# Cache copies, head states and the first output-projection weights in a hybrid decoder step

## The chip, the cores and the metric

The kernel runs on one core of a Trainium2 chip. The metric is the device time of one execution in microseconds (us). Before the change three runs gave 789.93, 790.48 and 792.44 us; the median is 790.48 us.

## The reference, cut to what matters

One layer is computed for 512 prompt tokens (one sequence) and for 8 sampled tokens (8 sequences with 1024 cached tokens each), with 1024 model dimensions and float32 results.

```python
sh_a, sc_a, gt_a, sh_f, sc_f, gt_f = adaln(c, w_ada[l], b_ada[l])
h = rms_norm(x, g_pre_mix[l]) * (1.0 + sc_a) + sh_a
parts = split_projection(h @ w_in[l])
o_nsa, o_hgrn, states = mixer(parts, l)
mixed = jnp.concatenate([rms_norm(o_nsa, g_nsa_out[l]), o_hgrn], axis=-1) @ w_out[l]
x = x + gt_a * rms_norm(mixed, g_post_mix[l])
h = rms_norm(x, g_pre_ffn[l]) * (1.0 + sc_f) + sh_f
ffn = hier_moe(h, w_route_group[l], b_route_group[l], ...)
x = x + gt_f * rms_norm(ffn, g_post_ffn[l])
```

`mixer` is two things side by side. `o_nsa` is a sparse attention with 8 heads of 64 (a compressed, a selected and a window branch, summed with gates). `o_hgrn` is a gated linear recurrence with 4 heads and a 128 x 128 state each, whose final state is an output. The window cache of the 8 sampled sequences is an output too: it is the old one moved on by one row. So 511 of its 512 rows per sequence are a plain copy, 511 KB for each of 8 sequences:

```python
kw = jnp.concatenate([win_buf, kv_w.astype(win_buf.dtype)], axis=1)
return nsa_combine(gates, o_c, o_s, o_w), kw[:, t:]
```

`hier_moe` sends each token to 2 of 16 experts, each a gated MLP with 256 hidden columns.

## The kernel before, in words

The program has stages in this order: modulation and norms, input projection, recurrence inputs and attention scores, the mixing proper, output projection, residual and router, routing, experts, final norm. A float32 product is made of three products of rounded numbers: each operand is split into a high part (a copy on ScalarE, ACT in the profile) and a low part (a subtraction, mostly on VectorE, DVE, some on GpSimd, POOL); `split`, L111 to L113, does that, and its two instructions carry the lines L112 and L113 wherever they are called.

The change lies in the mixing and in the start of the output projection.

**The mixing** (from about 330 to 447 us) runs several generators. Each `next` issues one step of one of them, and a string gives the order: `ORD_D`, then `ORD_F`, then `ORD_E`.

- `mix(h)`, h = 0 to 3, letters 4 to 7: one head of the recurrence over the prompt. It builds the state tile `S` (128 x 4 x 128, one for each of 4 chunks), L997 to L1000, stores the last one (`O["ph"]`, L1001, a DMA on SyncE's queue), multiplies with it (L1008), normalizes (L1011 to L1018; `hq` holds the head's output) and transposes the result into `mixT` (L1022, L1023).
- `attn(i)`, i = 0 to 3, letters a to d: attention of 128 prompt tokens. Scores go to the two PSUM tiles `mm`, their exponentials to a ring of three SBUF tiles `PT` (L1055), the values are summed in `ob` (L1066). At the end the squares of `ob` go to a tile `sqt` of its own (L1077, L1078), and four matmuls with ones sum them (L1081); the output is written as high and low parts `mh` (L1088, L1089).
- `hgrn_samples`, letter h: the recurrence of the 8 samples. It writes the values to DRAM (`HV`, L1107), reads them back broadcast to all partitions (`VB`, 2 MB, L1108), and updates the state tiles `S0` (printed as S too; L1102, L1125) two samples at a time. The last step normalizes `osn` and transposes it (L1146).
- `copy_windows`, letter w: the eight cache copies, one a step, DRAM to DRAM on SyncE's queue (L711).

**The output projection** (from L1171) takes `w_out` in eight tiles of 128 x 1024, 512 KB each. Tiles 0 to 3 hold the first 512 output columns, 4 to 7 the second 512. `load_wout` (L1174 to L1177) issues one load on SyncE's queue, into one of six slots `ewr0` to `ewr5` of the pool `wpa`, or later into `ewr6` to `ewr9` of the pool `res`. `wpa` is opened after the mixing's own pools (`hgo` with `hq`, `hl`, `hv`; `hmx`) are closed, at the same place in SBUF. `wout_half` (L1185) splits four tiles: the high part goes to `ewh` (first half) or `ewi` (second half), the low part to another slot. `first_half`, letter f in `ORD_E`, splits the first four, then loads tiles 4 and 5 into slots 2 and 3, then splits the four heads of `mixT` into `mhh`. Tiles 6 and 7 are loaded after `res` is opened. `wout` (L1269, matmuls at L1277) computes 128 tokens by 512 columns in 24 matmuls; `wout_samples` (L1290) the samples. `router_weights` (L1323 to L1350) prepares the router in small matmuls. `ORD_W` gives the order of these.

**What sets the order.** Outside of a few stretches that are written out by hand (routing and experts), the program's order is only a priority: a planner simulates the program with its own costs and sets the order of each engine's instructions. Each engine then runs its list in order. Transfers are issued by SyncE (SP) and by ACT, in order too; an issue that must wait holds up all behind it. `tc.keep_in_program_order` pins an instruction: what comes before it in the program on that engine is issued before it, and what comes after it is issued after it. A tile pool gives out tiles by name; `bufs` is how many a name has in rotation, and a tile may be written when all readers of what was in its place are done. DMA completions are told by eight semaphores that are given out in turn, over both queues.

Of the kernel before, what the change touches and what calls it, by code (L numbers as in the profile page):

```python
# [11 lines left out]
F32 = mybir.dt.float32  # L12
# [10 lines left out]
D = 1024  # L23
# [32 lines left out]
ORD_C = "PPPrPsPrPPrPsPrPPsPrPPrPsPrPPrsPPPrPsPrPPrttsPPrPPrsPPPrsPPrPPrsPPrPsPPrPPrsPPrttPsPrPPrPsPPrPsPrPPrPsPrPPsPrPPrPsPrttPPrsPPrPPsPrPPrsPPrPPrsPPPrsPPPPsPPPsPPPPPPPPPtt"  # L56
ORD_D = "gvvvvgvvvvgvvvv4vvvvv4vvvvv45vvvvv45vvvvv456vvvvv"
ORD_E = "dhfdhfdhfdhfdhdhdhdhdhdhhhh"
ORD_F = "h456waaha456w7abhb56w7bbhb5w67bchc6w7ccwhc67wcchcw7h7h"
ENG = "aadaaaaaddddddddddddddppppppddppppppaaaaddddadaappppaaaadpddppppppppaaaadaaadddddddddpppaaapadddddpddpppd"  # L60
ORD_W = "ffhhrlhhhlrfrgggaaaaalfagfllllglalaala"
ORD_M = "GLAESSTBKSSSSGLAEFLSSTBBBBKSSSSGLAEFLSSTBKSSSSGLAEFLSSTBKSSSSGLAEFLSSTBKSSGLAEFLSSTBKSSGLAEFLSSTBKGLAEFLSSTBKSSGLAEFLSSTKSSSSGLAEFLSSTKSSSSGLAEFLSSTKSSSSGLAEFLSSTKSSSSGLAEFLSSTKSSSSGLAEFLSSTKSSSSGLAEFLSSTKSSSSGLAEFLSSTKSSSSGLAEFLSSTKGLAEFLTK"
# [2 lines left out]
def body(tc, I, O):  # L65
    nc = tc.nc
    es = ExitStack()
    dve, act, pool, pe, sp = nc.vector, nc.scalar, nc.gpsimd, nc.tensor, nc.sync

    def stage():  # L70
        return es.enter_context(ExitStack())

    def open_pool(name, bufs, stack, side="left"):
        return stack.enter_context(tc.tile_pool(name=name, bufs=bufs, side=side, reuse_waits=REUSE))
# [13 lines left out]
    def ps_mm():  # L88
        return bank("mm", 2, 512)
# [7 lines left out]
    def ps_t():  # L97
        return bank("pt", 512)

    def ps_o():  # L100
        return bank("po", 512)
# [9 lines left out]
    def split(src, hi, lo, eng=None):  # L111
        act.activation(hi, src, AF.Copy)  # L112
        (eng or dve).tensor_tensor(lo, src, hi.bitcast(F32), op=ALU.subtract)  # L113
# [4 lines left out]
    def copied(i, dst, src):  # L118
        if ENG[i] == "a":
            act.activation(dst, src, AF.Copy)  # L120
        else:
            en(i).tensor_copy(dst, src)
# [585 lines left out]

    def copy_windows():
        for b in range(8):  # L710
            tc.keep_in_program_order(sp.dma_start(O["sw"][b], I["cwo"][b]))  # L711
            yield

    def drained(gens):
        for c, g in gens.items():
            assert next(g, self_end) is self_end, c
# [16 lines left out]
    def sample_attention():  # L733
# [50 lines left out]
        for r in range(2):  # L784
# [26 lines left out]
            for q in range(2):  # L811
                S = ps_t()
                for bb in range(4):
                    pe.matmul(S[32 * bb:32 * bb + 32, :], qb[:, 4 * r + bb, :], SLK[bb][:, 4 * q:4 * q + 4, :], start=True, stop=True)
                dve.tensor_tensor(P[:, 512 * q:512 * q + 512], S, ts[:, 512 * q:512 * q + 512], op=ALU.add)
            W = ps_t()
# [71 lines left out]
    hmx = open_pool("hmx", 1, s_hm)  # L888
# [52 lines left out]
    def mix(h):  # L941
# [52 lines left out]
        pk = ps_f()  # L994
        for c in range(4):
            pe.matmul(pk[:, 128 * c:128 * c + 128], KT_[:, c], hv[:, c, 128 * h:128 * h + 128], start=True, stop=True)
        S = hmx.tile([128, 4, 128], F32, name="S")  # L997
        copied(40 + h, S[:, 0], pk[:, 0:128])
        for c in range(1, 4):
            dve.scalar_tensor_tensor(S[:, c], S[:, c - 1], EB[:, c:c + 1], pk[:, 128 * c:128 * c + 128], op0=ALU.mult, op1=ALU.add)  # L1000
        sp.dma_start(O["ph"][:, h], S[:, 3])  # L1001
        yield
        po = ps_f()
        for c in range(4):
            o = po[:, 128 * c:128 * c + 128]
# [21 lines left out]
    gens = dict(v=hgrn_values(), g=gated_raw(), **{"4567"[h]: mx4[h] for h in range(4)})  # L1027
# [7 lines left out]
    s_at = stage()  # L1035
    at = open_pool("at", 1, s_at, "right")
# [4 lines left out]
    def attn(i):  # L1041
        qc = slice(128 * i, 128 * i + 128)
        ob = ps_o()
        last = []
        for h in range(8):
            o = ob[64 * (h % 2):64 * (h % 2) + 64, 128 * (h // 2):128 * (h // 2) + 128]
            pe.matmul(o, Vb[:, h // 4, h % 4, :], pcT[:, i, h // 4, :], start=(h < 2), stop=False)
        for g in range(2):
            def scores(n, j):
                S = ps_mm()  # L1050
                for br in range(2):
                    pe.matmul(S[:, br], AK[:, i, i - j], AG[:, 8 * br + 4 * g:8 * br + 4 * g + 4], start=True, stop=False)
                    for q in range(2):
                        pe.matmul(S[:, br], KS[g][:, q, br, j], QS[g][:, :, qc], start=False, stop=(q == 1))  # L1054
                PT = at.tile([128, 2, 4, 128], F32, name="PT", bufs=3)  # L1055
                S4 = S.rearrange("p b (h q) -> p b h q", h=4)
                for h in range(4):
                    act.activation(PT[:, :, h], S4[:, :, h], AF.Exp, scale=-SL[4 * g + h])  # L1058
                if n == 0:
                    pool.affine_select(out=PT, in_=PT, compare_op=ALU.is_ge, fill=0.0, base=0, pattern=[[0, 8], [1, 128]], channel_multiplier=-1)  # L1060
                return PT, g, j, n

            def values(PT, g, j, n):
                for br in range(2):
                    for par in range(2):
                        pe.matmul(ob[64 * par:64 * par + 64, 256 * g:256 * g + 256], VT[:, j, br, 64 * g:64 * g + 64],  # L1066
                                  PT[:, br].rearrange("p (r t) q -> p t r q", t=2)[:, par], start=False, stop=(n == i and br == 1 and g == 1))

            for n, j in enumerate([i, *range(i)]):
                s_ = scores(n, j)  # L1070
                if last:
                    values(*last.pop())
                last.append(s_)
                yield
        values(*last.pop())
        yield
        sqt = at.tile([128, 4, 128], F32, name="sqt")  # L1077
        act.activation(sqt, ob.rearrange("p (f q) -> p f q", f=4), AF.Square)  # L1078
        ps = ps_t()
        for f in range(4):  # L1080
            pe.matmul(ps[:, 0:1], sqt[:, f], ones[:, 0:1], start=(f == 0), stop=(f == 3))  # L1081
        copied(80 + i, ssn[:, i:i + 1], ps[:, 0:1])
        for f in range(4):
            src = ob[:, 128 * f:128 * f + 128]
            if ENG[76 + i] == "a":
                act.activation(mhi[f][:, qc], src, AF.Copy, scale=gn[:, f:f + 1])
            else:
                dve.tensor_scalar(mhi[f][:, qc], src, gn[:, f:f + 1], None, op0=ALU.mult)  # L1088
            dve.scalar_tensor_tensor(mlo[f][:, qc], src, gn[:, f:f + 1], mhi[f][:, qc].bitcast(F32), op0=ALU.mult, op1=ALU.subtract)  # L1089
        yield  # L1090
# [58 lines left out]

    hs = hgrn_samples()
    gens.update(h=hs, w=copy_windows(), **{"abcd"[i]: attn(i) for i in range(4)})
    with contextlib.ExitStack() as order:
        if DMAN:
            order.enter_context(tc.manual_schedule(engines={pe.engine}))
        for c in ORD_F:
            next(gens[c], None)
        drained({c: gens[c] for c in "abcw4567"})
        s_hm.close()  # L1160
        s_hg.close()

        wpa = open_pool("wpa", 1, es)
        slot = [lambda dt, c=c: wpa.tile([128, D], dt, name=f"ewr{c}") for c in range(6)]
        hslot = [lambda dt, c=c: wpa.tile([128, D], dt, name=f"ewh{c}") for c in range(4)]
        high = [h(F32R) for h in hslot]
        mh2 = [wpa.tile([128, D], F32R, name=f"mhh{c}") for c in range(4)]
        mhh, mlh = ([mh2[2 * q + h // 2][:, 512 * (h % 2):512 * (h % 2) + 512] for h in range(4)] for q in range(2))  # L1170
        KKS = (2, 3, 0, 1)  # L1171
        raw = []

        def load_wout(s_):  # L1174
            c = len(raw)
            raw.append(slot[s_](F32))
            sp.dma_start(raw[c], I["wo"][c // 4, KKS[c % 4]])  # L1177

        for c in range(4):
            load_wout(c)  # L1180

        def halves(x):
            return x.rearrange("p (a b) -> p a b", a=2)

        def wout_half(hf, wh, wl):  # L1185
            for q, kk in enumerate(KKS):
                c = 4 * hf + q
                lo = slot[(4, 5, 0, 1, 8, 9, 2, 3)[c]](F32R)
                split(raw[c], high[c], lo, en(93 + c))
                wh[kk], wl[kk] = halves(high[c]), halves(lo)  # L1190
                yield

        ws, wt2 = ([None] * 4, [None] * 4), ([None] * 4, [None] * 4)

        def first_half():
            for _ in wout_half(0, *ws):
                pass
            yield
            load_wout(2)
            load_wout(3)  # L1200
            for h in range(4):
                split(mixT[4 + h][:, 0:NP], mhh[h], mlh[h], en(101 + h))
                yield

        fh = first_half()
        play(ORD_E, h=hs, d=gens["d"], f=fh)
    s_at.close()
# [26 lines left out]
    high += [res.tile([128, D], F32R, name=f"ewi{c}") for c in range(4)]  # L1234
    slot += [lambda dt, c=c: res.tile([128, D], dt, name=f"ewr{c}") for c in range(6, 10)]
    ring = [gslot, *slot[6:8], *slot[0:2], *slot[4:6], *hslot, *slot[2:4]]
    load_wout(6)
    load_wout(7)
    loaded = []

    def load_next():
# [163 lines left out]
    raws, parts, at, used = {}, {}, {}, set()  # L1405
# [335 lines left out]
    with tc.manual_schedule(engines=MANUAL and {getattr(nc, e).engine for e in MANUAL}):  # L1741
# [5 lines left out]
        for o in ORD_M:  # L1747
            u = k[o] if o in k else 0
            if o in k:
                k[o] += 1  # L1750
                w, c = units[min(u, len(units) - 1)]
# [230 lines left out]
```

## Time and profile before

| what | value |
| --- | --- |
| median of three runs | 790.48 us |
| the profiled execution's own time | 791.27 us |
| its span, first to last instruction | 789.6 us |
| mean granted TensorE clock | 0.92 |
| TensorE busy, of the span | 651.7 us (83%) |
| VectorE, ScalarE, GpSimd busy | 464.0, 374.1, 183.3 us |
| moved by DMA | 160.81 MB, mean 204 GB/s |
| SyncE's queue | 125.98 MB, 46.6% of 16 engines' span |
| ScalarE's queue | 25.39 MB, 9.9% |
| the eight cache copies issued | from 359.7 to 456.4 us |
| the eight loads of w_out issued | from 462.1 to 475.9 us |

Times in the profile count from the first instruction of the span. "PE" is a matmul, "PEld" the load of its stationary operand, "SPq" and "ACTq" the issue of a transfer on that engine's queue. In a timeline each row gives the start, how long it took, the engine, the line, the operation, what it writes and reads, and in brackets how long the engine was idle before it and what ended that wait. A float32 matmul shows as two instructions. Rows of waits give what waited, for what, the total, how often, and the longest. The wait of an instruction for several things is put down to the last of them.

### The profile page before, as it was taken

The numbers are of one execution on the slowest core, as the hardware profiler recorded it, in microseconds if no ns is written. First come the engines' busy times: TensorE is split into PE (matmuls) and PEld (weight loads), VectorE is DVE, ScalarE is ACT, GpSimd is POOL, SyncE is SP. The second block draws the span as 40 slices with busy tenths as digits, with TensorE's granted clock in tenths as the row PEclk, the third lists the DMA queues.
The fourth block names the chain that finished last, engine by engine and source line by source line (L and its number), as shares of the span: only waits on it lengthen the run. The fifth ranks groups of instructions, "written<-read, shape, count | busy, mean of one in ns | idle before, by whom it ended". The sixth has DMA issues, their size and how long they took to land. (4 is left out here: it accounts for less than half of the span.)

```text
span 789.6 us, 13169 instructions
## 1 busy us (share of the span) xinstructions
PE 651.7 (83%) x4495; PEld 490.3 (62%) x4495; DVE 464.0 (59%) x1140; ACT 374.1 (47%) x759; POOL 183.3 (23%) x208
## 2 busy tenths in 40 slices
PE   3885988998999999897999739995288899999930
PEld 1663866687878788885676426564255577666620
DVE  4523613345867765577643544356865976888806
ACT  4212512334455547623444234445445766888723
POOL 1000310002130131425432112435301223222114
PEclk9898999999999999999999958997588999999975
DMA  8876798866454632106221485338698889998515
GB/s 302 262 256 218 258 315 295 316 197 205 141 175 130 182 118 73 56 4 262 94 81 55 102 303 177 112 123 319 212 358 295 263 222 287 359 333 296 148 29 213
DMA packets 74604, 160.81 MB, mean 204 GB/s; under 512 B 11346, under 2 KB 39538, under 8 KB 74146
## 3 DMA queue, kind: packets, MB, share of 16 engines
q1 hardware_dynamic: 59844, 125.98, 46.6%
q10 hardware_dynamic: 10654, 25.39, 9.9%
q0 software_dynamic: 4032, 8.53, 5.1%
q8 instruction: 37, 0.61, 0.3%
q14 instruction: 37, 0.30, 0.1%
HBM read 145.29 MB, written 24.28 MB: 215 GB/s over the span
## 5 line engine op out<-in xcount | busy, mean ns | idle before, releaser
L563 PE MATMUL pp<-hhi,wh 128*128 128x260 f32 x256 | 75.6, 295 | 0.3 <-ACT kvt L441 0.3
L563 PE MATMUL pp<-hlo,wh 128*128 128x260 f32 x256 | 74.4, 291 | 0.0
L563 PE MATMUL pp<-hhi,wl 128*128 128x260 f32 x256 | 74.2, 290 | 0.0
L1669 POOL DMA_INDIRECT Y<-ot,gi x17 | 24.4, 1438 | 130.1 <-ACT ot L1668 123.0
L563 PEld LDWEIGHTS pp<-hhi,wh 128*128 128x128 f32 x256 | 49.4, 193 | 2.7 <-issue 2.0
L563 PEld LDWEIGHTS pp<-hhi,wl 128*128 128x128 f32 x256 | 49.3, 193 | 2.4 <-issue 2.3
L563 PEld LDWEIGHTS pp<-hlo,wh 128*128 128x128 f32 x256 | 49.4, 193 | 1.4 <-issue 1.2
L655 ACT ACTIVATE jn<-P,M 128x128 bf16<-128x128 f32 (+3 forms) x64 | 35.9, 560 | 27.3 <-DVE M L653 21.8
L113 DVE TENSOR_TENSOR wl<-wr,wh 128x1024 fp32r<-128x1024 f32 x9 | 11.2, 1250 | 39.8 <-ACT wh L112 39.8
L1058 ACT ACTIVATE PT<-mm 128x256 f32<-128x256 f32 x80 | 23.9, 388 | 19.8 <-PE mm L1054 19.7
L1640 PE MATMUL pf<-ewi,xh 128*96 128x512 f32 x72 | 30.2, 419 | 2.0 <-ACT xh L112 2.0
L653 DVE CUSTOM_DVE_ANT_0 P<-mm,tb 128x128 f32<-128x128 f32 (+3 forms) x64 | 29.0, 483 | 4.0 <-PE mm L646 3.9
L397 PE MATMUL mm<-hhi,wh 128*128 128x260 f32 x144 | 29.9, 288 | 1.3 <-ACT wh L112 1.3
L1640 PE MATMUL pf<-ewi,xl 128*96 128x512 f32 x72 | 29.5, 409 | 1.2 <-DVE xl L113 1.2
L112 ACT ACTIVATE wh<-wr 128x1024 fp32r<-128x1024 f32 x9 | 9.5, 1057 | 43.3 <-DMA wr<-in_wi 25.9
L397 PE MATMUL mm<-hlo,wh 128*128 128x260 f32 x144 | 30.0, 285 | 0.0
L397 PE MATMUL mm<-hhi,wl 128*128 128x260 f32 x144 | 29.7, 287 | 0.0
L646 PE MATMUL mm<-ka,qs 128*128 128x512 f32 (+2 forms) x112 | 27.6, 354 | 0.1
L1054 PE MATMUL mm<-qs,ka 128*128 128x512 f32 x80 | 26.6, 405 | 0.0
L1667 ACT ACTIVATE ot<-mm 96x512 f32<-96x512 f32 x17 | 10.1, 594 | 33.3 <-PE mm L1664 33.3
L397 PEld LDWEIGHTS mm<-hhi,wh 128*128 128x128 f32 x144 | 22.2, 188 | 5.0 <-issue 3.4
L299 PEld LDWEIGHTS po<-cg,w1c 128*128 128x128 f32 x160 | 21.5, 214 | 5.7 <-issue 3.3
(651 smaller groups left out, 1885.1 us busy)
## 6 DMA issues: line engine op xcount, KB each, us to landing
ewr<-in_ew SPq DMA_DIRECT2D x37, 512.0 KB
wa<-in_wa SPq DMA_DIRECT2D x16, 1024.0 KB
wr<-in_wi ACTq DMA_DIRECT2D x25, 512.0 KB
ewt<-in_ew SPq DMA_DIRECT2D x24, 512.0 KB
cg<-in_cc SPq DMA_DIRECT2D x64, 128.0 KB
ewh<-in_ew SPq DMA_DIRECT2D x16, 512.0 KB
x<-in_ew SPq DMA_DIRECT2D x15, 512.0 KB
mh<-in_wa SPq DMA_DIRECT2D x13, 512.0 KB
```

Of the source, the lines that this page charges most:

```text
L113: (eng or dve).tensor_tensor(lo, src, hi.bitcast(F32), op=ALU.subtract)
L299: pe.matmul(p[:, 128 * k:128 * k + 128], w1c[:, k, s, :], cg[:, :, k, s, :], start=(s == 0), stop=(s == 7))
L397: pe.matmul(p[:, hf, 0:260], a[:, k, :], b[:, k, hf * 260:hf * 260 + 260], start=(k == 0 and j == 0), stop=(k == KT - 1 and j == 2))
L563: pe.matmul(p[:, 0:260], a[:, k, :], b[:, k, c], start=(k == 0 and j == 0), stop=(k == KT - 1 and j == 2))
L646: pe.matmul(o, QS[g][:, h % 4, qc], KA[g][:, j, a:b], start=(j == 0), stop=(j == 1))
L653: dve.tensor_tensor_reduce(out=p, in0=sb[:, br], in1=tb0[:, 384 - 128 * i:512].rearrange("p (k n) -> p k n", n=128), scale=SL[h], scalar=1 ...
L655: act.activation(jn[:, 0:128 * (i + 1)], p.rearrange("p k n -> p (k n)"), AF.Exp, scale=-1.0, bias=M[:, 0, i, br, h:h + 1], accum_out=M[:, ...
L1054: pe.matmul(S[:, br], KS[g][:, q, br, j], QS[g][:, :, qc], start=False, stop=(q == 1))
L1058: act.activation(PT[:, :, h], S4[:, :, h], AF.Exp, scale=-SL[4 * g + h])
L1640: pe.matmul(pg, a[:, k, :], b[:, wk_], start=(k == 0 and j == 0), stop=(k == 7 and j == 2))
L1667: act.activation(o3[:, 0], pd[:, 0], AF.Copy)
L1669: pool.indirect_dma_start(out=Y, out_offset=bass.IndirectOffsetOnAxis(ap=gix, axis=0), in_=ot, in_offset=None, bounds_check=T - 1, oob_is_ ...
```

## The change

Three things are changed.

- The eight copies are no longer pinned; they stand at other places of `ORD_F`.
- The state tile `S` of `mix` has two buffers instead of one. The squares `sqt` of `attn` no longer have a tile: they take half of a `PT` tile, from its ring of three.
- The first four tiles of `w_out` get four tiles of their own (`wq0` to `wq3`, 4 KB a partition each, in a pool opened on the right side, above the attention's). They are loaded by a new generator `first_weights`, letter o, two in the second step of `ORD_F` and two in the twelfth. Tiles 4 and 5 are loaded into slots 2 and 3 as soon as `wpa` is open. The order of the letters 4 to 7, a, b, c and h among themselves is the same.

```diff
--- before.py
+++ after.py
@@ -56,7 +56,7 @@
...
 ORD_D = "gvvvvgvvvvgvvvv4vvvvv4vvvvv45vvvvv45vvvvv456vvvvv"
 ORD_E = "dhfdhfdhfdhfdhdhdhdhdhdhhhh"
-ORD_F = "h456waaha456w7abhb56w7bbhb5w67bchc6w7ccwhc67wcchcw7h7h"
+ORD_F = "ho456aaha45ow67awwbhb567wwbbhb567bwwchc67wwcchc67cchc7h7h"
 ENG = "aadaaaaaddddddddddddddppppppddppppppaaaaddddadaappppaaaadpddppppppppaaaadaaadddddddddpppaaapadddddpddpppd"
 ORD_W = "ffhhrlhhhlrfrgggaaaaalfagfllllglalaala"
 ORD_M = "GLAESSTBKSSSSGLAEFLSSTBBBBKSSSSGLAEFLSSTBKSSSSGLAEFLSSTBKSSSSGLAEFLSSTBKSSGLAEFLSSTBKSSGLAEFLSSTBKGLAEFLSSTBKSSGLAEFLSSTKSSSSGLAEFLSSTKSSSSGLAEFLSSTKSSSSGLAEFLSSTKSSSSGLAEFLSSTKSSSSGLAEFLSSTKSSSSGLAEFLSSTKSSSSGLAEFLSSTKSSSSGLAEFLSSTKGLAEFLTK"
@@ -708,7 +708,7 @@
 
     def copy_windows():
         for b in range(8):
-            tc.keep_in_program_order(sp.dma_start(O["sw"][b], I["cwo"][b]))
+            sp.dma_start(O["sw"][b], I["cwo"][b])
             yield
 
     def drained(gens):
@@ -994,7 +994,7 @@
         pk = ps_f()
         for c in range(4):
             pe.matmul(pk[:, 128 * c:128 * c + 128], KT_[:, c], hv[:, c, 128 * h:128 * h + 128], start=True, stop=True)
-        S = hmx.tile([128, 4, 128], F32, name="S")
+        S = hmx.tile([128, 4, 128], F32, name="S", bufs=2)
         copied(40 + h, S[:, 0], pk[:, 0:128])
         for c in range(1, 4):
             dve.scalar_tensor_tensor(S[:, c], S[:, c - 1], EB[:, c:c + 1], pk[:, 128 * c:128 * c + 128], op0=ALU.mult, op1=ALU.add)
@@ -1074,7 +1074,7 @@
                 yield
         values(*last.pop())
         yield
-        sqt = at.tile([128, 4, 128], F32, name="sqt")
+        sqt = at.tile([128, 2, 4, 128], F32, name="PT", bufs=3)[:, 0]
         act.activation(sqt, ob.rearrange("p (f q) -> p f q", f=4), AF.Square)
         ps = ps_t()
         for f in range(4):
@@ -1149,14 +1149,29 @@
 
 
 
+    raw = []
+    KKS = (2, 3, 0, 1)
+
+    def load_wout(t_):
+        c = len(raw)
+        raw.append(t_)
+        sp.dma_start(t_, I["wo"][c // 4, KKS[c % 4]])
+
+    def first_weights():
+        wq = open_pool("wq", 1, s_at, "right")
+        for c in range(4):
+            load_wout(wq.tile([128, D], F32, name=f"wq{c}"))
+            if c % 2:
+                yield
+
     hs = hgrn_samples()
-    gens.update(h=hs, w=copy_windows(), **{"abcd"[i]: attn(i) for i in range(4)})
+    gens.update(h=hs, o=first_weights(), w=copy_windows(), **{"abcd"[i]: attn(i) for i in range(4)})
     with contextlib.ExitStack() as order:
         if DMAN:
             order.enter_context(tc.manual_schedule(engines={pe.engine}))
         for c in ORD_F:
             next(gens[c], None)
-        drained({c: gens[c] for c in "abcw4567"})
+        drained({c: gens[c] for c in "abcow4567"})
         s_hm.close()
         s_hg.close()
 
@@ -1168,16 +1183,8 @@
         high = [h(F32R) for h in hslot]
         mh2 = [wpa.tile([128, D], F32R, name=f"mhh{c}") for c in range(4)]
         mhh, mlh = ([mh2[2 * q + h // 2][:, 512 * (h % 2):512 * (h % 2) + 512] for h in range(4)] for q in range(2))
-        KKS = (2, 3, 0, 1)
-        raw = []
-
-        def load_wout(s_):
-            c = len(raw)
-            raw.append(slot[s_](F32))
-            sp.dma_start(raw[c], I["wo"][c // 4, KKS[c % 4]])
-
-        for c in range(4):
-            load_wout(c)
+        load_wout(slot[2](F32))
+        load_wout(slot[3](F32))
 
         def halves(x):
             return x.rearrange("p (a b) -> p a b", a=2)
@@ -1196,8 +1203,6 @@
             for _ in wout_half(0, *ws):
                 pass
             yield
-            load_wout(2)
-            load_wout(3)
             for h in range(4):
                 split(mixT[4 + h][:, 0:NP], mhh[h], mlh[h], en(101 + h))
                 yield
@@ -1234,8 +1239,8 @@
     high += [res.tile([128, D], F32R, name=f"ewi{c}") for c in range(4)]
     slot += [lambda dt, c=c: res.tile([128, D], dt, name=f"ewr{c}") for c in range(6, 10)]
     ring = [gslot, *slot[6:8], *slot[0:2], *slot[4:6], *hslot, *slot[2:4]]
-    load_wout(6)
-    load_wout(7)
+    load_wout(slot[6](F32))
+    load_wout(slot[7](F32))
     loaded = []
 
     def load_next():
```

## The prediction

> **What bounds the kernel now.** I began with the page: it says which stage has slack on TensorE, and what clock it was granted there.
>
> ```profile
> PE   3885988998999999897999739995288899999930
> PEclk9898999999999999999999958997588999999975
> DMA  8876798866454632106221485338698889998515
> ```
>
> A slice is 19.7 us. TensorE is nearly full except where the page shows a hole near 455 to 475 us (the 3 in the PE row, a 5 in the clock row) and a second one at the routing. To read the first hole I asked for stretches.
>
> ```profile
> 430.00:440.00 10.00, 10.00 (x57) 6.40 (x56) 0.60 (x1) 4.23 (x13) 2.13 (x2) 1.00 0.00 0
> 440.00:450.00 10.00, 5.70 (x53) 2.71 (x52) 7.41 (x33) 3.37 (x11) 1.18 (x9) 1.00 0.48 109
> 450.00:460.00 10.00, 8.23 (x67) 6.65 (x67) 5.14 (x30) 2.99 (x6) 1.65 (x2) 0.56 0.70 191
> 460.00:470.00 10.00, 1.46 (x4) 0.60 (x4) 3.11 (x7) 1.08 (x2) 2.25 (x2) 0.50 1.02 346
> ```
>
> The columns are PE, PEld, DVE, ACT, POOL, granted clock, DMA share and GB/s. From 430 to 440 the DMA engines move nothing; from 460 to 470 they are full and every compute engine is nearly idle. Work that could have been fetched earlier is fetched while all wait. The timeline names it.
>
> ```profile
> 445.43 0.33 PE L1022 MATMUL pt<-ident,hq 128*128 128x128 f32 x1
> ...
> 450.86 0.30 PE L1146 MATMUL pt<-ident,osn 128*128 128x128 f32 x1 [3.61 <-DVE osn L1143]
> ...
> 451.16 0.34 SPq L1001 DMA_DIRECT2D out_ph<-S  x1
> 451.54 5.41 SPq L711 DMA_DIRECT2D out_sw<-in_cwo  x2
> ...
> 460.11 0.24 PE L1331 MATMUL po<-sel,lT 128*8 128x20 f32 x2 [0.29 <-DVE lT L1330]
> ...
> 462.13 14.09 SPq L1177 DMA_DIRECT2D ewr<-in_wo  x8
> ...
> 467.52 1.06 ACT L112 ACTIVATE ewh<-ewr 128x1024 fp32r<-128x1024 f32 x1 [7.69 <-DMA ewr<-in_wo]
> 468.63 1.22 PE L1277 MATMUL mm<-ewh,mhh 128*128 128x512 f32 x2 [8.28 <-ACT ewh L112]
> ...
> 471.24 4.62 DVE L113 TENSOR_TENSOR ewr<-ewr,ewh 128x1024 fp32r<-128x1024 f32 x4
> ...
> 472.52 0.80 PE L1277 MATMUL mm<-ewr,mhh 128*128 128x512 f32 x1 [2.67 <-DVE ewr L113]
> ```
>
> The mixing ends near 446, small router matmuls run from 450.86 to 460.35, and then the output projection (L1277) waits 8.28 us for its first weight tile and 2.67 us for the low part of it. The queue's own waits say why the eight loads come only at 462.13.
>
> ```profile
> SPq L1001 <- DMA tab<-MOD: 40.8, 1, 40.8
> ...
> SPq L1177 <- DMA Y<-zero: 10.4, 4, 5.0
> SPq L711 <- DMA out_sw<-in_cwo: 4.4, 1, 4.4
> SPq L1108 <- DMA HV<-hvs: 2.9, 1, 2.9
> ```
>
> SyncE issues in order. The last head-state store stood 40.8 us at its head, waiting for the landing of a table load with which it shares no data (an issue here waits for an earlier DMA of its completion semaphore). Two pinned cache copies stood behind it, and the weight loads behind those; they then waited 10.4 us more for zero fills.
>
> **The change part by part.** *First four weight tiles.* They get tiles of their own and are issued from the second step of the last mixing phase. Added: no load; four 512 KB loads move from 462 to about 360 to 390. They can start there: the last readers of the old projection buffers that I take to lie under them are turned at the end of 354, in the first row below, and the DMA engines have room in the second and third.
>
> ```profile
> 354.58 0.44 PE L929 MATMUL pt<-ident,kvt 128*128 128x128 f32 x2 [0.30 <-DVE kvt L566]
> 360.00:370.00 10.00, 5.72 (x34) 4.35 (x31) 9.65 (x27) 4.21 (x13) 6.74 (x7) 0.97 0.66 263
> 380.00:390.00 10.00, 9.86 (x98) 7.30 (x91) 8.61 (x34) 5.07 (x16) 2.96 (x4) 1.00 0.14 54
> ```
>
> At 263 GB/s, 2.1 MB take 8 us, with 55 us to spare until 446. On SyncE they pass the head-state stores and the copies; if one waits for its space, only those stand behind it, and no engine waits for those. What is late next is the split of those tiles. I take its targets to need the space of the head outputs (`hq`), read last by the transpose that starts at 445.43 and takes 0.33 us. Four high parts on ACT are 4 x 1.06 us, so 450.0, before the 450.86 at which TensorE has other work. Four low parts on DVE are 4.62 us together and follow one by one. So I remove the whole **8.28** (bounds 0, were the loads no earlier, to 8.28) and the whole **2.67**; the bound of the second is -2.67, when a low part is as late behind its high part again as now. I take the full removal because the projection uses the tiles one after another and the router matmuls stand between.
>
> *Clock.* The next rows are the first projection matmuls and the same ones later.
>
> ```profile
> 472.52:478.22 5.70, 5.70 (x13) 4.51 (x14) 3.35 (x3) 3.18 (x4) 0.00 (x0) 0.50 0.74 265
> 486.52:496.74 10.22, 10.22 (x45) 8.01 (x44) 2.63 (x5) 2.53 (x6) 3.28 (x2) 1.00 0.31 103
> ```
>
> 13 matmuls took 5.70 us at clock 0.50; at 10.22/45 = 0.227 us each they take 2.95. That is at most 2.75 us, and 0 if another hole puts the same ramp elsewhere. The 3.61 us hole before L1146 stays in my sum, so I take half, **1.4**. The Trainium skill (TensorE: Matmul & The Clock Gate, "What's actually happening") has the clock halved after an idle window of about 3.4 us and restored after about as long a busy one; the trace agrees in kind (1.00 until 450, 0.50 to 0.56 until 478). By that rule alone the 3.61 us hole would keep a ramp, no clock gain would be left, and the sum would be 10.95 instead of 12.35.
>
> *What could come on top.* If the planner sets projection matmuls before L1146, up to 3.61 us more; if the router stretch (9.49 us at clock 0.56) runs at full clock, some 2.8 us, since eight of its transposes take 1.95 there and 1.38 later:
>
> ```profile
> 452.31 1.95 PE L1323 MATMUL pt<-ident,tab 128*128 128x128 f32 x8
> ...
> 522.97 1.38 PE L1323 MATMUL pt<-ident,x 128*128 128x128 f32 x8
> ```
>
> I take 0 for both and keep them for the low end.
>
> *Copies freed.* The eight copies lose their pin and move within the mixing in program order. No instruction is added; each issue costs SyncE half a microsecond, and SyncE is idle from 410 to 451. The next row has the eight issues.
>
> ```profile
> L711 SPq DMA_DIRECT2D out_sw<-in_cwo x8: 509/522/1387, 359.7 to 456.4; - x8
> ```
>
> I take 0: they lie beside the mixing, where DMA is at 0.00 to 0.66. Bounded by -4.4 (the copy's own wait above, if two still stand ahead of weight loads) and +0; the gain of the unpinning is already in the 8.28.
>
> *Two state buffers, and the squares in the probabilities' ring.* No wait of a state write for its store is in the trace; the squares wait only for TensorE, as the first row shows, and their readers (second row) follow within 10 us. Cost 0. Were a slot of the ring still held by squares not yet summed, ACT's next exponentials would stand behind it and TensorE behind those; the worst I find beside it is the 3.2 us of the sums' readers, so -3.2 to 0.
>
> ```profile
>   PE po L1066: 7.6, 4
>   DVE ssn L122: 3.2, 4
> ```
>
> *Fifth and sixth tile.* They are loaded as soon as their slots are free instead of after the third and fourth tile are split; the seventh and eighth as before. 0 in the sum, a rival below.
>
> **Sum**: 8.28 + 2.67 + 1.4 = 12.35 us. The profiled execution has 791.27 us (span 789.6 and 1.7 around it), 0.79 above the median of 790.48, so 778.9 for it and **778.1** for the median.
>
> Does it reach the end? After the hole TensorE is full, then routing is a serial chain, then the experts:
>
> ```profile
> 558.90 0.20 PE L1490 MATMUL po<-C,tri 128*128 128x16 bf16 x1 [11.76 <-DVE C L1486]
> 600.00:755.00 155.00, 147.84 (x726) 103.88 (x724) 122.00 (x170) 111.50 (x172) 34.06 (x27) 1.00 0.85 264
> PE pt L1652 <- DVE xl L113: 6.4, 6, 1.7
> SPq L1415 <- PE pf L1640: 42.5, 32, 8.9
> ```
>
> In the experts TensorE is busy 147.84 of 155 us, waits 6.4 us and never for a load; the loads wait 42.5 us for TensorE to free slots. So an earlier start moves all of it.
>
> **The rivals.** The first needs the row where the second half of the projection begins.
>
> ```profile
> 491.05 0.40 PE L1277 MATMUL mm<-ewi,mhh 128*128 128x512 f32 x1
> ```
>
> *A, the second half's weights are the new wait (783.5).* If tiles five to eight still queue behind zero fills and table loads, they go out as the first four did, 462.13 to about 469, or as late as 476. The second half starts 18.5 us after the first (472.52, and the row above), so with the first starting at 457 to 460 it wants its weights near 475 to 479, while the last tile issued at 476 lands and is split some 7 us later (462.13 to 468.6 for the first). That leaves 4 to 8 us of stall; with 5.4, 783.5. For it: the 10.4 us of waits on zero fills. Against: two of the four no longer wait for a split. The Trainium skill (DMA: Bandwidth & Descriptors, "Issuing engines are not separate DMA queues") adds that loads from both queues share the same 16 engines; the full 1.02 share beside the zero fills agrees.
>
> *B, absorbed (789.5).* The experts get no weights earlier, because DMA, at 0.85, is the real limit there. Then only routing ends sooner. Against: the two waits above. This is also where I put "it doesn't do what it says", with the early loads planned behind the last state store after all.
>
> *C, slower (797).* SyncE waits 2.9 us for HV before the 2 MB broadcast VB. If freed copies and weight loads go out in that wait, two loads and four copies (0.52 MB read each, copies written too: 5.1 MB) take 19.5 us at 263 GB/s. DVE's first use of VB is
>
> ```profile
> 370.04 0.34 DVE L1125 SCALAR_TENSOR_TENSOR S<-VB,hsn,S 128x128 f32<-128x128 f32 x1
> ```
>
> and DVE is in order, with all mixing steps behind it. Above 12.35 us of delay it is slower; at 19.5, 778.1 + 19.5 = 797.6. Against: the program puts copies behind the second pair of loads, so two loads (4 us) are likelier ahead.
>
> *D, better (771).* Both extras above, 3.61 + 2.8, come too.
>
> **Chances.** Forecast 0.54, A 0.23, B 0.08, C 0.09, D 0.06. The range leaves out C and most of B above, and the far end of D below (12.35 + 2.75 - 1.4 + 3.61 + 2.8 = 20.1, so 770.4): 770 to 788.5. About 0.3%, 2.4 us, is what this kernel's measurements tell from no change; faster is forecast, A and D (0.83), same is B (0.08), slower is C (0.09).
>
> **What would show it.** Right: the first w_out loads land long before 440; no wait of ACT's high parts on them; the first L1277 matmul between 450 and 461, dense from there; L1490 near 546 to 547; the experts' stretch as long as now. Wrong: a new wait of L1277 on the ewi tiles (A), L1125 later than 374 (C), or L1490 earlier but the experts' gaps ended by DMA (B).

## The result, and the profile after

The changed kernel takes **780.70 us** (median of 18 runs, 773.06 to 789.98), the kernel before 792.39 us in 18 runs of the same comparison (786.67 to 796.32). The ratio is 0.9845, 95% interval 0.9823 to 0.9868: about 12.3 us less. It leaves out the two slow runs of the changed kernel. Forecast were 778.1 us and 12.35 us less, in a range of 770 to 788.5.

The profiled execution after is the fastest of its 18 (773.06 us, span 771.3), so the two spans can't simply be subtracted. The first head-state store (`out_ph`, L1001) was issued at 354.13 us before and at 347.25 after: 6.88 us of the difference lie ahead of the mixing's last phase. I therefore count from that store, called **the mark** below. In the changed kernel the lines behind L1150 stand some 5 lines later: the projection's matmul is L1282 (was L1277), routing begins at L1495 (was L1490).

The page of the changed kernel, in slices of 19.3 us:

```profile
PE   3886998998999989897999899992579899999930
PEclk9998999999999999998999999997598999999975
DMA  8887789856454645207332172378697889998415
```

The hole that stood near 455 to 475 us before (3 in the PE row, 5 in the clock row) is gone; the one at routing is still there. From the mark to the first matmul of routing, in windows of the kernel before and of the changed one (columns: length, then busy time of PE, PEld, DVE, ACT and POOL, granted clock, DMA share, GB/s):

```profile
354.13:558.90 204.77, 164.97 (x1121) 112.59 (x1119) 109.21 (x286) 81.55 (x196) 72.91 (x61) 0.88 0.49 168
```

```profile
347.25:538.74 191.49, 163.01 (x1120) 109.19 (x1119) 110.32 (x286) 80.33 (x196) 74.05 (x61) 0.93 0.49 169
440.00:450.00 10.00, 7.69 (x32) 3.27 (x31) 5.71 (x6) 6.31 (x13) 6.40 (x12) 0.83 0.60 217
450.00:460.00 10.00, 10.00 (x62) 6.24 (x62) 4.50 (x25) 0.00 (x0) 0.00 (x0) 1.00 0.94 293
460.00:470.00 10.00, 10.00 (x55) 6.94 (x54) 4.34 (x8) 6.69 (x10) 2.47 (x1) 1.00 0.40 102
```

The stretch is 13.28 us shorter. TensorE's idle time in it fell from 39.80 (204.77 - 164.97) to 28.48 us, by 11.32; its busy time, at 0.93 instead of 0.88 of the clock, by 1.96. From there to the end it is 230.7 us before (789.6 - 558.90) and 232.6 after (771.3 - 538.74): 1.9 us are given back. The timeline of the changed kernel shows what fills the hole:

```profile
348.28 0.34 SPq L1158 DMA_DIRECT2D wq<-in_wo  x1
...
407.24 0.34 SPq L1001 DMA_DIRECT2D out_ph<-S  x1
...
438.37 3.90 ACT L112 ACTIVATE ewh<-wq 128x1024 fp32r<-128x1024 f32 x4
...
443.02 1.65 PE L1295 MATMUL pf<-ewr,msn 128*32 128x512 f32 x2 [2.31 <-DVE ewr L113]
446.31 2.14 PE L1066 MATMUL po<-PT,VT 128*64 128x256 f32 x14
448.38 0.50 PE L1282 MATMUL mm<-ewh,mhh 128*128 128x512 f32 x1
...
448.57 0.38 ACTq L1306 DMA_DIRECT2D tab<-MOD  x1
...
458.64 1.09 PE L1328 MATMUL pt<-ident,tab 128*128 128x128 f32 x8
...
538.74 0.19 PE L1495 MATMUL po<-C,tri 128*128 128x16 bf16 x1 [12.66 <-DVE C L1491]
```

Three things are to be seen. The first weight tile is on its way at 348.28. The last head-state store goes out 60.0 us after the mark (407.24), where it was 97.0 (451.16). And the order of the work is another one: the projection's first large matmul (L1282) starts at 448.38 without a wait, 101.1 us after the mark instead of 114.5, and the router's tables are turned (L1328) only at 458.64, inside the projection. Before, all of the router's small matmuls stood between the mixing and the projection. The longest of the store's waits on SyncE's queue answers to the row with 40.8 us of before; no table stands in it any more:

```profile
SPq L1001 <- DVE S L1000: 91.7, 4, 43.9
```

The store now waits for its own data. The cache copies have partly moved out of the mixing altogether, the first to 291.7 us:

```profile
L711 SPq DMA_DIRECT2D out_sw<-in_cwo x8: 509/582/1435, 291.7 to 386.5; - x8
```

One wait of the same kind is left, and there it costs nothing: an expert load waits for a constant of ScalarE's queue, but its own place comes free only 10.6 us after that, as the second row says:

```profile
SPq L1249 <- DMA kon<-in_kon: 16.8, 1, 16.8
SPq L1249 <- DVE cW L1345: 10.6, 1, 10.6
```

### The profile page after: what moved, and what is told of

It reads as the page before. It is cut to its first block, busy times and chain, and to the rows that moved or that the text cites. A ratio compares the mean times of both kernels' runs of the same rounds, so it can differ in the third digit from the quotient of the medians.

```text
span 771.3 us, 13171 instructions
## 1 busy us (share of the span) xinstructions
PE 648.9 (84%) x4495; PEld 484.8 (63%) x4495; DVE 465.1 (60%) x1140; ACT 372.8 (48%) x759; POOL 184.0 (24%) x208
## 5 line engine op out<-in xcount | busy, mean ns | idle before, releaser
L1620 POOL DMA_INDIRECT XG<-H,gi x18 | 18.5, 1030 | 28.4 <-PE pt L1633 14.0
```

Of the source, the lines that this page charges most:

```text
L1620: pool.indirect_dma_start(out=xg, out_offset=None, in_=H2, in_offset=bass.IndirectOffsetOnAxis(ap=gix, axis=0), bounds_check=T - 1, oob_is ...
```

## The experiments

The result leaves two readings. By **theory 1**, the one of the prediction, the early landing of the first four weight tiles is the gain, and the unpinning only lets them go. By **theory 2** it is enough that nothing is pinned in SyncE's queue. Twelve kernels were run, each timed in five rounds beside the kernel before on the same chip. The table gives what all of them have to say; all times but the waits are in us after the mark, from the timelines. "Foreign wait" is the longest wait, after the mark, of a head-state store, a cache copy or a w_out load for a transfer of ScalarE's queue that shares no data with it ("none": none over 1 us).

| kernel | time / before, 95% | foreign wait | last state store | 4th w_out load | first projection matmul | last residual load | routing |
| --- | --- | --- | --- | --- | --- | --- | --- |
| before | 1 | 40.8 (tables) | 97.0 | 114.6 | 114.5 | 169.9 | 204.8 |
| after | 0.9845 [0.9823, 0.9868] | none | 60.0 | 16.4 | 101.1 | 156.2 | 191.5 |
| e1 | 1.0025 [0.9993, 1.0056] | 68.0 (tables) | 109.4 | 16.4 | 116.5 | 172.0 | 207.0 |
| e2 | 0.9858 [0.9805, 0.9911] | none | 63.9 | 73.2 | 98.5 | 156.2 | 191.6 |
| e3 | 0.9842 [0.9795, 0.9888] | 2.6 (a state store, a load waits) | 64.6 | 66.4 | 97.4 | 153.5 | 188.9 |
| e4 | 0.9834 [0.9781, 0.9886] | none | 64.0 | 73.2 | 101.9 | 158.9 | 194.7 |
| e5 | 1.0319 [1.0263, 1.0374] | 79.1 (tables) | 113.6 | 122.3 | 132.7 | 190.2 | 225.4 |
| e6 | 1.0142 [1.0092, 1.0192] | 48.3 (zeros) | 105.3 | 116.3 | 120.8 | 173.1 | 208.4 |
| e7 | 1.0124 [1.0080, 1.0167] | 78.8 (zeros) | 121.4 | 16.3 | 110.6 | 171.0 | 205.2 |
| e8 | 1.0049 [1.0009, 1.0089] | 65.3 (zeros) | 58.7 | 116.8 | 121.6 | 174.5 | 209.8 |
| e9 | 1.0050 [1.0021, 1.0079] | 10.8 (a state load, a copy waits) | 75.5 | 89.2 | 102.2 | 179.8 | 206.5 |
| e10 | 1.0269 [1.0221, 1.0316] | 16.1 (a constant) | 75.0 | 111.5 | 120.8 | 199.0 | 222.8 |
| e11 | 0.9893 [0.9855, 0.9931] | none | 64.9 | 74.4 | 101.2 | 161.2 | 195.4 |
| e12 | 1.0038 [1.0003, 1.0074] | 13.8 (zeros, a copy waits) | 60.2 | 70.6 | 96.3 | 179.4 | 208.5 |

**e1, the change with its copies pinned again.** Early weights and two state buffers stay.

```diff
-            sp.dma_start(O["sw"][b], I["cwo"][b])
+            tc.keep_in_program_order(sp.dma_start(O["sw"][b], I["cwo"][b]))
```

> The changed kernel with its eight cache copies pinned in program order again; the early weight loads and the two state buffers stay. Theory 1 (the gain is that the first four weight tiles have landed before the mixing ends): the early loads are issued in the mixing as before, so the ratio to the kernel before stays at 0.985 within 0.003, and no wait of the projection's first high part on its load appears. Theory 2 (the gain is that nothing pinned stands in SyncE's queue any more): the last state store again stands at the queue's head, the later loads wait for it, and most of the gain is lost, 0.995 or more.

1.0025: no difference from before that can be measured. The first four weight tiles are issued just as early as in the changed kernel (16.4 us after the mark), and no time is gained. Its waits and timeline:

```profile
SPq L711 <- DMA tab<-MOD: 68.0, 1, 68.0
```

```profile
395.21 69.70 SPq L711 DMA_DIRECT2D out_sw<-in_cwo  x3
...
457.94 1.94 PE L1328 MATMUL pt<-ident,tab 128*128 128x128 f32 x8 [4.08 <-DMA tab<-MOD]
...
465.02 0.53 SPq L1001 DMA_DIRECT2D out_ph<-S  x1
...
467.61 3.90 ACT L112 ACTIVATE ewh<-wq 128x1024 fp32r<-128x1024 f32 x4 [0.56 <-PE pt L1328]
...
472.08 0.80 PE L1282 MATMUL mm<-ewh,mhh 128*128 128x512 f32 x1 [1.94 <-ACT mhh L112]
```

A pinned copy waits 68.0 us for a table load of ScalarE, the last state store stands behind it until 465.02, and ScalarE splits the tiles only at 467.61, 95.6 us after the last of them was issued, behind the router's transposes (the row's bracket). So the early weights do take away the 8.28 and 2.67 us of before. But the router's work still comes ahead of the projection on TensorE, and TensorE now waits for the router's loads instead: 4.08 us for a table and 4.31 us for the router's weights, then 1.94 us ahead of the first L1282 matmul.

**e2, everything but the early weights; e3, the early weights issued at the end of the mixing; e4, only the pin removed from the kernel before.**

```diff
-ORD_F = "h456waaha456w7abhb56w7bbhb5w67bchc6w7ccwhc67wcchcw7h7h"
+ORD_F = "h456aaha45w67awwbhb567wwbbhb567bwwchc67wwcchc67cchc7h7h"
```

```diff
-ORD_F = "ho456aaha45ow67awwbhb567wwbbhb567bwwchc67wwcchc67cchc7h7h"
+ORD_F = "h456aaha45w67awwbhb567wwbbhb567bwwchc67wwcchc67cchc7h7hooo"
```

The first is e2 (in the kernel before, with the copies free, `S` in two buffers and the squares in the `PT` ring), the second e3 (in the changed kernel). e4 is e1's diff read backwards, in the kernel before.

> The kernel before with free copies at the changed places, two state buffers and the squares in the probabilities' ring, but all eight weight tiles loaded where they were. Theory 1: the loads can start only when the slots under the head outputs are free, near the end of the mixing; the wait for them shrinks from 8.3 us to some 4 to 6, so the ratio is 0.990 to 0.996. Theory 2: the queue is free, all of the gain is there, 0.985 within 0.003.

> The changed kernel with the letter o moved to the end of the mixing's string: the four tiles have their own place, but are issued last of the mixing's loads. Theory 1: what counts is when they land; the planner issues them near the last state store, and if that is well before the mixing ends the ratio is the changed kernel's, 0.985 within 0.003; if they land after the mixing ends it is near 0.992. Theory 2: 0.985 in both cases.

> The kernel before with one edit: the pin of the copies is gone. Theory 1: 0.990 to 0.996, with the wait of the first high part on its load at 4 to 6 us. Theory 2: 0.985 within 0.003 and no such wait.

0.9858, 0.9842 and 0.9834, with intervals that overlap each other and that of the change. e3 alone decides nothing: its early weights, issued 65.0 to 66.4 us after the mark, are in time by either theory. e1, e2 and e4 decide: theory 1 falls, theory 2 holds, and **one removed pin gives all of the gain that can be measured**. In e4's timeline:

```profile
418.07 0.34 SPq L1001 DMA_DIRECT2D out_ph<-S  x1
...
425.87 24.90 SPq L1177 DMA_DIRECT2D ewr<-in_wo  x6
...
442.65 1.08 ACT L112 ACTIVATE ewh<-ewr 128x1024 fp32r<-128x1024 f32 x1
...
455.95 0.50 PE L1277 MATMUL mm<-ewh,mhh 128*128 128x512 f32 x1
```

The state store is out at 418.07, the weights follow from 425.87 into their old slots, and they are split from 442.65, 13.3 us ahead of the first matmul. The weights still have to be there in time; but they needn't come at 350, and they need no place of their own: once the copies are free, the loads go out 36 us earlier than before by themselves (the first 71.8 us after the mark instead of 108.0).

**What makes the pin cost so much?** e5 puts the pinned copies where the program starts its last phase. e6 and e7 take the state store's hold off the tile `S`; e8 takes the store off SyncE's queue.

```diff
-ORD_F = "h456waaha456w7abhb56w7bbhb5w67bchc6w7ccwhc67wcchcw7h7h"
+ORD_F = "wwwwwwwwh456aaha4567abhb567bbhb567bchc67cchc67cchc7h7h"
```

```diff
-        sp.dma_start(O["ph"][:, h], S[:, 3])
+        sf = sm.tile([128, 128], F32, name="sf", bufs=1)
+        dve.tensor_copy(sf, S[:, 3])
+        sp.dma_start(O["ph"][:, h], sf)
```

```diff
-        sp.dma_start(O["ph"][:, h], S[:, 3])
+        act.dma_start(O["ph"][:, h], S[:, 3])
```

The second is e6 in the kernel before and e7 in e1; the third is e8.

> The kernel before with one edit: all eight cache copies stay pinned, but stand at the head of the mixing's last phase, right after the first head-state store. Theory P (place: a pinned copy costs only because the last head-state store and the weight loads have to stay behind it): nothing is pinned behind the first 30 us of the phase any more, so the gain comes back, ratio 0.983 to 0.988, about 781 us; ScalarE's high parts of w_out stand between the exponentials of the last attention block, as with free copies. Theory Q (a pin as such costs, for instance because 8 MB read and written in a row hold up HV and VB): about 1.00, or slower if DVE's first use of VB comes later than with free copies (372 us or so).

> The kernel before with one edit: the last state chunk is copied on DVE to a small tile of its own (four copies of 128 x 128 in all) and stored from there, so that the late store no longer holds the state tile S; copies pinned as before. Theory M (memory: the late store keeps the place that the projection's tiles need): the slots are free at the end of the mixing, but the loads still stand behind the pinned copies and the store in SyncE's queue, so little or nothing, 0.997 to 1.003. Theory O (order: what stands behind the pinned copies in SyncE's queue is late, whatever it holds): the same, 1.00. This run alone doesn't tell the two apart; with the next it does.

> The kernel after with two edits: copies pinned again (as in e1, which took 1.0025 of the time before), and the last state chunk copied on DVE to a small tile of its own and stored from there. The first four weight tiles are loaded early, so neither the loads nor the held place of S keeps the splits waiting. Theory M: the splits of w_out no longer wait for the store (at 465.02 in e1, splits from 467.61), so most of the gain comes back, 0.985 to 0.991. Theory O: the planner still places the splits behind the router's work on ScalarE, as its list for this kernel has them, and the time stays at 0.998 to 1.004.

> The kernel before with one edit: the four head-state stores are issued on ScalarE's queue, the copies stay pinned on SyncE's. Theory O (the store's place behind pinned copies is what costs): the store goes out when S is ready and the place is free, but ScalarE's high parts still stand behind the table loads in the planner's list; the loads come earlier than 462, and part of the 12 us comes back, 0.988 to 0.997. Theory M: the place is free at the end of the mixing, all of it comes back, 0.983 to 0.988. If the pinned copies themselves hold the loads back: 1.00.

None regains the time; e5, e6 and e7 are slower by 1% to 3%, and e6 and e7 lie outside the ranges of both of their theories. The longest waits of SyncE's queue for a foreign transfer are, for e5, e6, e7 and e8 in this order:

```profile
SPq L711 <- DMA tab<-MOD: 79.1, 1, 79.1
```

```profile
SPq L1003 <- DMA Y<-zero: 48.3, 1, 48.3
```

```profile
SPq L711 <- DMA Y<-zero: 78.8, 1, 78.8
```

```profile
SPq L711 <- DMA Y<-zero: 65.3, 1, 65.3
```

In each, one issue in SyncE's queue again waits for a transfer that ScalarE issues only 78.0 to 116.4 us after the mark; only the issue that is held changes. In e5 it is a copy with everything else of the phase behind it, HV and the second state store too, so TensorE waits in the middle of the recurrence:

```profile
454.89 1.22 PE L1006 MATMUL pf<-hv,AT 128*128 128x128 f32 x4 [14.91 <-DVE S L1000]
```

In e8 the store is out early (58.7 after the mark), but a copy waits 65.3 us and holds the weights until 114.5. In e7, where early weights and freed `S` come together, the projection starts 5.9 us earlier than in e1 (110.6 against 116.5), which points to the held tile as a part of it; routing is only 1.8 us earlier, and the ratio is worse than e1's (1.0124 against 1.0025). The profiled execution of e7 (793.33 us) is below its median of 800.18, and it doesn't show what makes that median slower. In e6 the waits explain a small part only: its profiled span is 13.9 us longer than that of before, 9.1 of them ahead of the mark and 3.7 between mark and routing; what lengthens the stretch ahead is not known.

In these kernels the completion semaphores go round over both queues, and an issue waits for the transfer that had its semaphore before: in each of the six traces with a wait of 40.8 to 79.1 us (before, e1, e5 to e8), the issue that waits and the transfer that it waits for carry the same semaphore. The Trainium skill (DMA: Bandwidth & Descriptors, "Anatomy of one DMA — SWDGE (gpsimd) path") says that the wait for a semaphore happens on the issuing sequencer, ahead of dispatch, and not in the DMA engines; the trace agrees, since in e8 one more copy and the eight weight loads stand still behind the copy that waits 65.3 us; the page says it of GpSimd's path, and here SyncE's is seen. The same page ("Issuing engines are not separate DMA queues") has it that issuing from several engines only saves issue time. In the kernel before, issuing from two engines also brought a wait of 40.8 us; that one queue for all would be faster is not shown (e9, e11).

**e9, e10, e12: pins kept, the foreign wait taken away or moved.** In e9 the router's loads, the zero fills and two constants go from ScalarE's queue to SyncE's; in e10 they stay and are pinned too; in e12 the pinned copies stand behind the w_out loads. e11 is e9 with the copies free.

```diff
-        act.dma_start(tab, m4[g, j, :, 8, :].unsqueeze(0).to_broadcast([128, 2, 512]))
+        sp.dma_start(tab, m4[g, j, :, 8, :].unsqueeze(0).to_broadcast([128, 2, 512]))
```

```diff
     load_next()
+    for _ in copy_windows():
+        pass
     act.dma_start(kon, I["kon"])
```

The first is e9 (and so for L1233, L1247, L1248, L1305, L1309, L1311, L1313), the second e12, with the letters w taken out of `ORD_F`.

> The kernel before, copies pinned at their old places, one edit: the router's loads, the zero fills and two constants (L1233, L1247, L1248, L1301 to L1313) are issued on SyncE's queue and no longer on ScalarE's. Theory R (false wait: the completion semaphores go round over both queues, so a pinned SyncE issue can be made to wait for a load on ScalarE's queue that ScalarE reaches only after the mixing; 40.8 us before, 68.0, 79.1, 78.8, 65.3 and 48.3 us in e1, e5, e7, e8 and e6): no SyncE issue waits over 20 us in the mixing, the last head-state store goes out when S is ready (before 430), the weights right behind, and the gain of about 12 us comes back with all pins in place: ratio 0.980 to 0.990. Theory P2 (the pin itself costs, because it holds the weight loads behind eight copies): at most a few us, 0.994 to 1.005.

> The kernel before, copies pinned at their old places, one edit: the same loads stay on ScalarE's queue but are pinned too, so that the planner can't put them ahead of SyncE's last copies and store. Theory R: the last store waits for no table or zero fill, so most of the gain comes back; the zero fills now stand ahead of ScalarE's high parts and beside the weight loads, which costs a few us, so ratio 0.982 to 0.993. Theory P2: 0.997 to 1.005. That ScalarE's table loads belong on another queue, and not that their turn was wrong: e9 fast and this one at 1.00.

> Copies free as in e4 (0.983) and the loads on SyncE's queue as in e9: what both are worth together. Theory R: the two edits take away the same wait, so they don't add up: 0.978 to 0.987, within 4 us of e4. If the loads on ScalarE's queue cost something beside that wait (about half a microsecond of its time for each of 14 issues): 0.972 to 0.978.

> The kernel before with one edit: the eight copies stay pinned, but stand after the eight w_out loads and the first expert load in the program instead of in the mixing. Theory L (place: what costs is that the last head-state store and the weight loads stand behind pinned copies, on the chip and in the planner's forecast, which then puts the router's 34 small matmuls ahead of the projection): the first projection matmul starts about 98 to 102 us after the first head-state store, as in the kernels with free copies (97.4 to 101.9; before 114.5; from the traces), routing (L1490) about 190 to 196 us after it, and the time is 0.982 to 0.990 of before; if the copies' 4.2 MB read and as much written then hold up expert loads, up to 0.995. Theory Q (a pinned transfer costs wherever it stands): 0.998 to 1.010.

e9 and e12 do at the start of the projection what was expected: the last store goes out 75.5 and 60.2 us after the mark, and the first projection matmul comes at 102.2 and 96.3 instead of 114.5. But they take 1.0050 and 1.0038, so theories R and L, by which the gain comes back, fail; the two times lie in the ranges of P2 and Q, and e10's lies above all of its ranges. The time is lost again between the projection's start and routing. e9:

```profile
447.31 1.79 SPq L1177 DMA_DIRECT2D ewr<-in_wo  x4
...
466.72 0.80 PE L1277 MATMUL mm<-ewr,mhh 128*128 128x512 f32 x1 [3.81 <-DVE ewr L113]
...
539.36 0.92 SPq L1356 DMA_DIRECT2D xr<-in_xp  x1
548.67 1.41 DVE L1369 SCALAR_TENSOR_TENSOR x<-mg,ssa,xr 128x512 f32<-128x512 f32 x2 [5.59 <-DMA xr<-in_xp]
549.57 1.72 PE L1323 MATMUL pt<-ident,x 128*128 128x128 f32 x7 [6.77 <-DVE x L1369]
```

and e12, whose lines behind L1246 stand two later:

```profile
454.56 0.49 PE L1279 MATMUL mm<-ewh,mhh 128*128 128x512 f32 x1
...
537.69 0.70 SPq L1358 DMA_DIRECT2D xr<-in_xp  x1
544.82 1.41 DVE L1371 SCALAR_TENSOR_TENSOR x<-mg,ssa,xr 128x512 f32<-128x512 f32 x2 [6.14 <-DMA xr<-in_xp]
545.72 1.51 PE L1325 MATMUL pt<-ident,x 128*128 128x128 f32 x6 [10.98 <-DVE x L1371]
```

The residual's last rows (`xr`) are loaded on SyncE's queue 179.8 and 179.4 us after the mark, 153.5 to 158.9 in the change and e2 to e4; the residual waits for them, and TensorE for the residual, 6.77 and 10.98 us, just ahead of routing. That is a part of the loss. From the first projection matmul to routing it is 90.4 us in the change, 104.3 in e9 and 112.2 in e12. TensorE idles there 10.5 and 16.6 us longer than in the change, of which these waits are 6.77 and 10.98, and its work takes 3.5 and 5.3 us longer, at a granted clock of 0.84 and 0.82 instead of 0.93. Without its one long wait e12 would reach routing near 197.5 (208.5 - 10.98), an estimate that wasn't run. In e10 the foreign wait only moves on, to the weight loads:

```profile
SPq L1177 <- DMA kpos<-in_kpos: 16.1, 1, 16.1
...
SPq L1177 <- DMA tab<-MOD: 9.8, 3, 4.1
```

e11 shows that the two cures don't add up: 0.9893, above its expected 0.978 to 0.987 and not better than e4.

So the long foreign wait goes with a late start of the projection, and without it (e9, e12) the start is early; but it isn't the whole price of the pin: no kernel with pinned copies got the time back. Each had something late in SyncE's queue, at the head of the projection or at its end. Why the planner finds an order without either only when the copies are free is in no trace, and stays open. So removing the pin is shown as the cause of the gain; by which steps the pin costs 12 us is shown in part.

## Why the prediction was right, and where it wasn't

**The place and the size came out right.** The wait of 8.28 us for the first weight tile and the 2.67 us for its low part are gone: the first L1282 matmul has no wait. Foretold were 10.95 us less idle time and 1.4 us of clock; measured are 11.32 and 1.96 from the mark to routing. Counted from the mark before (6.88 us added), the first projection matmul stands at 455.3 (foretold 450 to 461) and routing at 545.6 (546 to 547). The experts' weight loads never became the limit: no wait of TensorE from routing on is put down to a load, and the 1.9 us given back lie within routing, experts and tail.

**The step that failed is "First four weight tiles", which credits 8.28 + 2.67 to their early loads.** With those loads alone (e1) the gain is nothing (1.0025); without them (e2, e4) it is all there (0.9858, 0.9834). The prediction had seen the 40.8 us of the store behind a table load, and wrote "the gain of the unpinning is already in the 8.28": it took the wait as a delay of the loads and no more, so that an early load would get round it. e1 shows two things in its place. A wait in the queue doesn't stay with the instruction it was read at (it grew to 68.0 us and held a copy, and through it the store); and with it ScalarE's splits and the projection come behind the router in the order of the engines (first projection matmul 116.5 us after the mark, first router product 108.6; in e4 101.9 and 122.3). The copies' row, "I take 0", was the row with the gain. That the sum came out nonetheless is luck as far as the account goes: the change held the one edit that does remove both waits, and the prediction credited their removal to another.

**The smaller rows.** Two state buffers and the squares in the `PT` ring cost and bring nothing that can be measured (e2 with them 0.9858, e4 without them 0.9834). Tiles 5 and 6: no TensorE wait on the `ewi` tiles, so rival A didn't come. Rival C, a late VB, came in small and delayed nothing that can be seen. DVE's first use of VB is 3.65 us later against the mark (before, in a row of the prediction, 370.04 - 354.13 = 15.91; after 366.81 - 347.25 = 19.56; counted from the mark before 373.7, just short of the 374 that was its sign), far from its 12.35, as only three weight loads stand ahead of VB and no copy:

```profile
349.51 0.84 SPq L1158 DMA_DIRECT2D wq<-in_wo  x2
354.43 0.33 SPq L1108 DMA_DIRECT2D VB<-HV  x1
...
366.81 0.34 DVE L1125 SCALAR_TENSOR_TENSOR S<-VB,hsn,S 128x128 f32<-128x128 f32 x1
```

**Extras.** The 3.61 us hole ahead of L1146, kept at 0, went too: attention's last block now runs until 448.45 and covers it. With it 14.56 us of waits are gone, but the idle time fell by 11.32, so some 3.2 us are new waits, all in all: 2.31 at L1295, 0.90 more at routing (12.66 against 11.76), and smaller ones that came and went. The sum held because two errors of about 3 us cancelled, and that is luck too. With the hole the reason to halve the clock's term went too: by the rule of the Trainium skill that the prediction weighed (TensorE: Matmul & The Clock Gate, "What's actually happening") no idle window, no halved clock. From 450 to 470 the trace agrees: the granted clock is 1.00 in both windows. Just ahead it doesn't: from 440 to 450 the clock is 0.83, where the only long hole is the 2.31 us at L1295, shorter than the rule's window of about 3.4 us.

## What to carry to other kernels

Where one queue's issue waits for another queue's transfer with which it shares nothing, ask first what put it behind that transfer. Feeding the starved engine by another way (earlier loads, a store from a copy, another queue) left the wait in the queue here, and it held the next issue instead. Taking the wait away with the pins kept (e9, e12) gave the early start, but not the time; only dropping the pins did. Where a planner sets the order, an edit's worth can't be read from the wait that it removes alone, since the order changes with it: compare the order of the work on the bound engine, from a mark ahead of the edit to one behind it. And with several edits in one change, the smallest of them is tried alone first: here dropping the pin was worth 12 us, the other two parts nothing that could be measured.

## What the runs showed of the hardware that was not expected

In six traces an issue on one queue waited 40.8 to 79.1 us for a transfer of the other queue with which it shared only a completion semaphore. A hole of 2.31 us on TensorE was followed by a lowered clock (0.83 from 440 to 450 in the changed kernel). And the stretch ahead of the mark took 347.25 to 363.23 us in the fourteen profiled executions, one of each kernel, a spread larger than the effect, so that spans of single executions couldn't be compared without a mark.
